# Both directions of a delta rule's block solution in one loop, its matmuls in 32x32 tiles by turns

## The chip, the cores and the metric

The kernel runs on one core of one Trainium2 chip. The metric is the device time of one execution in microseconds, from the first to the last instruction of the core, as the median of several runs.

## What is computed

Three blocks run one after the other on 256 tokens of 2048 channels. The first has a convolution, a chunked linear attention and an attention over a memory, the second a sparse attention, a gating unit and a wide layer, the third a latent attention and a delta rule in both directions of time. The change is in the third block's delta rule alone. Its core, per head of 64 channels, with 16 heads and 256 steps in each direction:

```python
def rwkv7_bidir_scan(r, w_f, w_b, k_f, k_b, v, kk, a_f, a_b):
    ...
    xs = (tm(r, r), tm(w_f, w_b), tm(k_f, k_b), tm(v, v), tm(-kk, -kk), tm(kk * a_f, kk * a_b))

    def step(st, inp):
        r_t, w_t, k_t, v_t, a_t, b_t = inp
        sa = jnp.einsum('dbhij,dbhj->dbhi', st, a_t)
        st = st * w_t[..., None, :] + sa[..., None] * b_t[..., None, :] + v_t[..., None] * k_t[..., None, :]
        y = jnp.einsum('dbhij,dbhj->dbhi', st, r_t)
        return st, y
    ...
    y = ys[:, 0] + ys[::-1, 1]
```

After it come a norm over each head, a bonus, a gate, and the layer `u_rwkv = (y_rwkv * silu(z_rwkv)) @ w_br_rwkv`.

## The kernel before, in words

**The main stream.** Nearly all of the work is linear layers. `run_stream` goes through their weights in a fixed order, in items of [128 rows, 512 columns]. ScalarE rounds an item to a high part `wh`, VectorE makes the remainder `wl`, and TensorE multiplies both with the high and low parts of the activations (`xh` and `xl`, of the rwkv results `yr0` and `yr1`) into the accumulators `acc`: three matmuls for each of the two blocks of 128 tokens, six an item. Six items' `wh` and `wl` exist at a time, and an item is split five items ahead of its matmuls (`LEAD`).

**Side work.** Everything else is written as generators ("sides") that give up control at each `yield`. Between the main products `pump` takes a step of each side whose last step should be through by then. What "should" means is set by the class `Issue`, a planner that runs at build time: it adds up, in microseconds of its own, what each engine has been given (a side matmul in 4-byte numbers costs `max(0.085, max(n, m) / 600 + 0.003)`). Before an item's matmuls `need` lets sides step on until the activations have been made by the planner's clock. So the order of every engine's instructions is fixed when the program is built; on the chip each engine takes its own in that order and waits where an operand is missing. A tile's results are evacuated (`finish`) before the next tile's `need`. Sides share four banks of PSUM (`bank`, `unbank`).

**The delta rule.** `job(g)` does 8 of the 16 heads, job 0 before job 1. Within blocks of 128 tokens the recurrence is a triangular system `u = w + (a b) u`, which is solved by four blocks of 32 tokens. `inverses` has made the inverses of the diagonal blocks (`J["tt"]`; the profile calls the tile `tl`), `scores` the products `ab`, and the state that enters the second block of 128 tokens is `zb`. `solve(J, d)` is one side for each direction `d`; both run at once and are interleaved by `pump`. For each of the direction's two blocks of 128 tokens (`n`), and each of the four blocks of 32 tokens in them (`e`, of quarter `q`):

- VectorE adds what earlier blocks gave (bank `pw`) to the rows `w` of `w0` (the profile calls it `w`);
- 8 matmuls, one a head, multiply `w` with the inverse into the quarter `q` of the bank `pu`, which both directions share under a lock per quarter; tile 32x32 at position (32 q, 32 q);
- ScalarE copies `pu` to `w`;
- `ab` products add the block's share to the quarters of `pw` still to come: in the first step (`e == 0`) two per head, one of 32 and one of 64 columns, in turn; in the second one of 64; in the third one of 32.

Between the two blocks of 128 tokens come 4 products with `bT` into another bank, which advance `zb`, and the flag `half`, for which `early` waits. `early` and `outputs` multiply the solution with `m` (tile `m0`), and `outputs` of job 1 norms, gates, transposes (`vy`) and splits the result into `yr1`. The main stream's layer `br1` (its first half, `br0`, takes job 0's `yr0`) is the first to read `yr1`.

Each engine instruction goes through one wrapper, so all have its line (283 before, 285 after).

Of the kernel before, what the change touches and what calls it, by code (L numbers as in the profile page):

```python
# [13 lines left out]
PSUM = bass.MemoryType.PSUM  # L14
AF = mybir.ActivationFunctionType
ALU = mybir.AluOpType
# [19 lines left out]
# tiles (the first so many of a layer) whose results come with the columns on the partitions:  # L36
# [128, 2, 256 tokens] in each of two banks
# [6 lines left out]
# ---------------------------------------------------------------- layout plan (shapes alone)  # L44
def stream_plan(blocks):
    """Tiles of the linear layers in the order in which they run:
    (key, j, source, first row, K chunks, first column, width)."""
# [63 lines left out]
class Narrow:  # L111
    """The result of a tile of a few columns, for which the weights are the stationary operand."""
# [5 lines left out]
def cut(plan):  # L118
    """Cuts the tiles into items of at most ITEM columns of SBUF, and these into DMA units."""
# [19 lines left out]
def col(v):  # L139
    """A vector over channels as [128, n / 128]."""  # L140
    return np.asarray(v).reshape(-1, 128).T


CVEC = {  # per-channel vectors, channel on the partition
# [33 lines left out]
ROWS = {  # vectors that are spread over the partitions  # L178
# [6 lines left out]
def shape_constants(block):  # L185
    """Constants of the shapes alone, [128, n] each."""
# [23 lines left out]
def bucket_onehot():  # L210
    """[32, 384]: the bucket of the distance 255 - c in column c; no bucket for negative distances."""
# [7 lines left out]
# ---------------------------------------------------------------- order of issue  # L219
class Issue:  # L220
    """Counts what each engine has been given (in microseconds, by the sizes of the operands), so that
    side work is issued between the main products about when its operands are there."""
# [16 lines left out]
    def take(self, eng, name, a, k):  # L239
# [3 lines left out]
        if eng == "PE":  # L243
# [3 lines left out]
            elif a[2].dtype == F32R:  # L247
                cost = max(n, 256) / 2400 + 0.003
            else:
                m = size(a[1])  # L250
                cost = max(0.085, max(n, m) / 600 + 0.003)
            self.t["PE"] += cost
# [42 lines left out]
# ---------------------------------------------------------------- the kernel  # L295
class Builder:
# [29 lines left out]
    # ---- memory  # L326
# [10 lines left out]
    def slotw(self, shape, name, keep=0, dtype=F32):  # L337
        """Side: a slot, once more than keep of them are free."""
# [14 lines left out]
    def keep(self, shape, name, dtype=F32):  # L353
        """A tile for as long as the block lasts."""
# [6 lines left out]
    def bank(self, n=1):  # L361
        """Waits for n banks of PSUM for side work, until they should have been read."""
# [2616 lines left out]
```

## Time and profile before

| | |
|---|---|
| median of 3 runs | 3649.19 us |
| lowest and highest | 3646.6 and 3651.16 us |
| span of the profiled execution | 3652.5 us |
| TensorE busy (matmul, weight load) | 3624.7 us (99%), 3110.4 us (85%) |
| VectorE, ScalarE, GpSimd busy | 67%, 52%, 4% |
| mean granted TensorE clock | 0.989 |

The profile is one execution of the program. Busy shares are means over the whole span, while the solution takes place in four stretches between 3072 and 3488 us: the first and the second block of 128 tokens of job 0 (3072 to 3114, 3125 to 3170), and those of job 1 (3388 to 3428, 3441 to 3488). What it costs there is read in the timeline.

### The profile page before, as it was taken

The page shows a single profiled execution, that of the slowest core. Times are in us where ns is not written, and L with a number is a line of the kernel's source. Part 1 is how long each engine was busy: PE and PEld are TensorE (multiplying, and loading weights), DVE is VectorE, ACT ScalarE, POOL GpSimd, SP SyncE. Part 2 cuts the span into 40 slices and gives each one's busy share as a digit, 9 for nine tenths or more (in the row PEclk, how much of TensorE's full clock was granted, in tenths as well). Part 3 has the DMA queues.
Part 4 walks back from the last instruction along what each step waited for, and adds up shares of the span by engine and source line. Part 5 has one row for each costly group of instructions (what it writes and reads, how often), then busy time and mean ns, then how long its engine had stood idle before and what let it go on. Part 6 is the DMA issues. An engine that isn't in the chain of part 4 may idle for free.

```text
span 3652.5 us, 56016 instructions
## 1 busy us (share of the span) xinstructions
PE 3624.7 (99%) x20498; PEld 3110.4 (85%) x20498; DVE 2453.4 (67%) x4453; ACT 1896.2 (52%) x3402; POOL 150.8 (4%) x141
## 2 busy tenths in 40 slices
PE   8999999999999999999999999999999999999998
PEld 7889988888988899888879898989888977877787
DVE  7598888886666665555855555555674786477485
ACT  6555556556544545655455454545555643353344
POOL 1000010010000001000200000000000000000010
PEclk9999999999999999999999999999999999999899
DMA  6555556676677665666755555555653555356365
GB/s 227 170 189 160 183 165 200 208 222 185 208 216 238 221 202 177 197 216 212 240 195 185 191 185 193 183 194 183 211 190 131 186 181 193 120 163 192 136 216 187
DMA packets 231772, 698.47 MB, mean 191 GB/s; under 512 B 40708, under 2 KB 51124, under 8 KB 229832
## 3 DMA queue, kind: packets, MB, share of 16 engines
q1 hardware_dynamic: 231496, 694.90, 58.9%
q8 instruction: 160, 2.62, 0.3%
q14 instruction: 116, 0.95, 0.1%
HBM read 661.22 MB, written 36.73 MB: 191 GB/s over the span
## 4 chain that ended last, share of the span: by engine, by line
PE 96%; DVE 2%; DMA 1%; ACT 1%; issue 0%; POOL 0%; SPq 0%; DVEq 0%; ACTq 0%
PE acc L283 85%; PE bank L283 11%; DVE wl L283 1%; DMA raw<-in_wstream_dram 1%; ACT wh L283 0%; DMA x<-f 0%; DMA sg<-z 0%; ACT junk L283 0%; DVE o L283 0%; DVE x L283 0%; DVE rsz L283 0%; DVE sg L283 0%; POOL mg L283 0%; SPq L283 0%; DVE mg L283 0%
## 5 line engine op out<-in xcount | busy, mean ns | idle before, releaser
L283 DVE TENSOR_TENSOR wl<-raw,wh 128x512 fp32r<-128x512 f32 x2290 | 1574.2, 703 | 1051.2 <-ACT wh L283 1037.9
L283 ACT ACTIVATE wh<-raw 128x512 fp32r<-128x512 f32 x2290 | 1424.0, 629 | 1553.5 <-PE acc L283 994.0
L283 PE MATMUL acc<-wh,xh 128*128 128x512 f32 x3328 | 1331.4, 400 | 8.5 <-ACT xh L283 5.0
L283 PE MATMUL acc<-wh,xl 128*128 128x512 f32 x3328 | 1302.2, 391 | 4.3 <-DVE xl L283 4.3
L283 PE MATMUL acc<-wl,xh 128*128 128x512 f32 x3328 | 1301.5, 391 | 0.9 <-DVE wl L283 0.9
L283 PEld LDWEIGHTS acc<-wh,xh 128*128 128x128 f32 x3328 | 629.1, 189 | 157.1 <-issue 21.0
L283 PEld LDWEIGHTS acc<-wh,xl 128*128 128x128 f32 x3328 | 628.7, 189 | 138.3 <-DVE xl L283 5.1
L283 PEld LDWEIGHTS acc<-wl,xh 128*128 128x128 f32 x3328 | 629.7, 189 | 124.6 <-DVE wl L283 2.5
L283 PE MATMUL acc<-xh,wh 128*128 128x256 f32 (+3 forms) x2224 | 637.3, 287 | 0.0
L283 PE MATMUL acc<-xh,wl 128*128 128x256 f32 (+3 forms) x2224 | 629.6, 283 | 0.0
L283 PE MATMUL acc<-xl,wh 128*128 128x256 f32 (+3 forms) x2224 | 629.5, 283 | 0.0
L283 PEld LDWEIGHTS acc<-xh,wh 128*128 128x128 f32 (+3 forms) x2224 | 423.9, 191 | 5.5 <-issue 4.0
L283 PEld LDWEIGHTS acc<-xl,wh 128*128 128x128 f32 (+3 forms) x2224 | 424.1, 191 | 1.1
L283 PEld LDWEIGHTS acc<-xh,wl 128*128 128x128 f32 (+3 forms) x2224 | 423.7, 191 | 0.4
L283 DVE SCALAR_TENSOR_TENSOR cacc<-u,cvec,cacc 128x226 f32<-128x226 f32 (+28 forms) x464 | 188.5, 468 | 0.0
L283 PE MATMUL bank<-ar,bk 64*128 64x128 f32 (+1 forms) x384 | 77.3, 328 | 0.0
L283 PEld LDWEIGHTS bank<-ar,bk 64*128 64x128 f32 x384 | 48.5, 186 | 19.3 <-issue 13.4
L283 ACT ACT_TABLE_LOAD x44 | 56.5, 1283 | 3.2 <-DVE mmx L283 1.6
L283 PE MATMUL bank<-w,ab 32*32 32x64 f32 (+1 forms) x512 | 54.5, 244 | 0.0
L283 PEld LDWEIGHTS bank<-w,ab 32*32 32x32 f32 (+1 forms) x512 | 38.6, 128 | 17.8 <-issue 6.2
L283 POOL TENSOR_TENSOR msh<-ev 128x508 f32<-128x508 f32 x8 | 10.1, 1261 | 1043.0 <-DVE ev L283 989.5
L283 ACT COPY w<-bank 32x512 f32<-32x512 f32 (+1 forms) x48 | 24.5, 511 | 50.7 <-PE bank L283 47.1
(420 smaller groups left out, 2292.0 us busy)
## 6 DMA issues: line engine op xcount, KB each, us to landing
raw<-in_wstream_dram SPq DMA_DIRECT2D x1133, 512.0 KB, 3.7
gate<-sg SPq DMA_DIRECT2D x40, 256.0 KB, 2.5
row<-in_rows_dram SPq DMA_DIRECT2D x38, 256.0 KB, 4.8
sg<-gate SPq DMA_DIRECT2D x24, 256.0 KB, 2.9
sg<-z SPq DMA_DIRECT2D x24, 256.0 KB, 3.0
z<-sg SPq DMA_DIRECT2D x20, 256.0 KB, 4.6
f<-x SPq DMA_DIRECT2D x16, 256.0 KB, 2.5
gt<-gate SPq DMA_DIRECT2D x16, 256.0 KB, 4.4
```

The source lines that it names most:

```text
L283: r = f(*a, **k)
```

## The change

`solve(J)` is one side for both directions. In each step the additions, products, copies and `ab` products of direction 0 and direction 1 are issued by turns; direction 0 works on quarter `e`, direction 1 on quarter `3 - e`. Each direction holds one bank `pw[d]` throughout: the products with the inverse go into the quarter of `pw[d]` that the addition has just read, and the state products into the same bank, so `pu`, its locks and `ps` go. Every `ab` product has a tile of 32x32, one per quarter still to come, and their group is cut in two in the first two steps. The flag `half` is set for both directions at once. The planner charges a matmul with a tile position half. Comments and docstrings were taken out too, which moves line numbers alone.

```diff
             else:
                 m = size(a[1])
                 cost = max(0.085, max(n, m) / 600 + 0.003)
+                if "tile_position" in k:
+                    cost /= 2
...
-            J["pu"], = yield from B.bank()
-            for d in range(2):
-                B.side(solve(J, d))
+            B.side(solve(J))
...
-            B.unbank(J["pu"])
...
-        def solve(J, d):
-            order = (0, 1) if d == 0 else (1, 0)
-            qs = (0, 1, 2, 3) if d == 0 else (3, 2, 1, 0)
-            ab, tt, w0 = J["ab"][d], J["tt"][d], J["w0"]
-            yield from B.wait(f"zb{d}{J['g']}")
-            zb, bT, pu = J["zb"][d], J["bT"][d], J["pu"]
-            for n, b in enumerate(order):
-                pw, = yield from B.bank()
...
-                for e, q in enumerate(qs):
-                    rows = slice(32 * q, 32 * q + 32)
-                    w = w0[rows, d, b]
+        def solve(J):
+            for d in range(2):
+                yield from B.wait(f"zb{d}{J['g']}")
+            ab, tt, w0, zb = J["ab"], J["tt"], J["w0"], J["zb"]
+            pw = yield from B.bank(2)
+            hs = [slice(h * 64, h * 64 + 64) for h in range(8)]
+            for n in range(2):
+                bs = (n, 1 - n)
...
+                for e in range(4):
+                    qs = (e, 3 - e)
+                    rows = [slice(32 * q, 32 * q + 32) for q in qs]
+                    ws = [w0[rows[d], d, bs[d]] for d in range(2)]
                     if n or e:
                         yield
-                        V.tensor_tensor(out=w, in0=pw[rows], in1=w, op=ALU.add)
+                        for d in range(2):
+                            V.tensor_tensor(out=ws[d], in0=pw[d][rows[d]], in1=ws[d], op=ALU.add)
                         yield
-                    yield from B.lock(f"pu{q}")
                     for h in range(8):
-                        T.matmul(pu[rows, h * 64:h * 64 + 64], tt[rows, 2 * h + b], w[:, h * 64:h * 64 + 64],
-                                 start=True, stop=True, tile_position=(32 * q, 32 * q))
-                    yield
-                    A.copy(out=w, in_=pu[rows])
-                    B.unlock(f"pu{q}")
-                    yield
-                    if e < 3:
-                        for h in range(8):
-                            for t0, m in ((32, 32), (64, 64)) if q == 0 else ((64, 32), (0, 64)) if q == 3 else (
-                                    ((64, 64),) if e == 1 and d == 0 else ((0, 64),) if e == 1 else
-                                    ((96, 32),) if d == 0 else ((0, 32),)):
-                                T.matmul(pw[t0:t0 + m, h * 64:h * 64 + 64], ab[rows, 2 * h + b, t0:t0 + m],
-                                         w[:, h * 64:h * 64 + 64], start=not n and e == 0 and h == 0, stop=e == 2,
-                                         tile_position=(32 * q, t0), skip_group_check=True)
-                B.unbank(pw)
+                        for d in range(2):
+                            T.matmul(pw[d][rows[d], hs[h]], tt[d][rows[d], 2 * h + bs[d]], ws[d][:, hs[h]], start=True,
+                                     stop=True, tile_position=(32 * qs[d], 32 * qs[d]), skip_group_check=True)
+                    yield
+                    for d in range(2):
+                        A.copy(out=ws[d], in_=pw[d][rows[d]])
+                    yield
+
+                    for h in range(8 if e < 3 else 0):
+                        if h == 4 and e < 2:
+                            yield
+                        for i in range(e + 1, 4):
+                            for d in range(2):
+                                t0 = 32 * (i, 3 - i)[d]
+                                T.matmul(pw[d][t0:t0 + 32, hs[h]], ab[d][rows[d], 2 * h + bs[d], t0:t0 + 32],
+                                         ws[d][:, hs[h]], start=not n and e == 0 and h == 0, stop=e == 2,
+                                         tile_position=(32 * qs[d], t0), skip_group_check=True)
                 if n == 0:
-                    ps, = yield from B.bank()
...
+                            T.matmul(pw[d][:, cs], J["bT"][d][:, cs], w0[:, d, d, cs], start=True, stop=True,
+                                     skip_group_check=True)
...
+            B.unbank(*pw)
+            J["done"] = [0, 1]
```

TensorE, first step of the solution's first block in job 0: the last main products ahead of the `ab` products (output, operands and output size; a name's number tells buffers apart). Before:

```order
L283 MATMUL acc_31066<-wh,xh 128x512
L283 MATMUL acc_31066<-wl,xh 128x512
L283 MATMUL acc_31066<-wh,xl 128x512
L283 MATMUL bank_31167<-w_29031,ab 32x64
L283 MATMUL bank_31167<-w_29031,ab 64x64
```
After:

```order
L285 MATMUL acc_31065<-wh,xh 128x512
L285 MATMUL acc_31065<-wl,xh 128x512
L285 MATMUL acc_31065<-wh,xl 128x512
L285 MATMUL bank_31166<-w_29031,ab 32x64
L285 MATMUL bank_31167<-w_29031,ab 32x64
```
Before, one direction's products of two sizes follow each other in one bank, eight pairs for each direction; now the two directions' banks take turns with products of one size, 24, three main products, and 24 more.

TensorE, end of job 1: the transposes of its normed results (`vy`) and the main products around them (`yr_33944` and `yr_33886` are job 0's half, `yr_35052` is job 1's). Before:

```order
L283 MATMUL acc_34828<-wl,yr_33944 128x512
L283 MATMUL acc_34828<-wh,yr_33944 128x512
L283 MATMUL bank_34862<-cst_80,vy 128x128 x4
L283 MATMUL acc_34827<-wh,yr_33944 128x512
L283 MATMUL acc_34827<-wl,yr_33944 128x512
L283 MATMUL acc_34827<-wh,yr_33944 128x512
```
After:

```order
L285 MATMUL acc_34962<-wh,yr_33886 128x512
L285 MATMUL acc_34962<-wl,yr_33886 128x512
L285 MATMUL acc_34962<-wh,yr_33886 128x512
L285 MATMUL bank_35054<-cst_80,vy 128x128 x4
L285 MATMUL bank_35061<-cst_80,vy 128x128 x4
L285 MATMUL acc_35068<-wh,yr_35052 128x512
```
The transposes of the two token blocks stood 9 main products apart, and 21 more products of job 0's half followed before the first of job 1's; now they stand together, straight ahead of the first product that reads `yr1`. From the last product with `m` to that one there were 147 main products, and there are 27.

VectorE at the same place: the first steps of the norm of job 1's results. Before:

```order
L283 TENSOR_TENSOR vy<-bank_34569,vy 128x512
L283 TENSOR_REDUCE yst<-vy 128x8
L283 TENSOR_SCALAR yst<-yst 128x8
L283 TENSOR_TENSOR wl<-raw,wh 128x512 x2
L283 TENSOR_TENSOR vy<-vy,yst 128x512
L283 TENSOR_TENSOR wl<-raw,wh 128x512
L283 TENSOR_TENSOR vy<-vy,yst 128x512
L283 TENSOR_TENSOR wl<-raw,wh 128x512 x2
L283 TENSOR_TENSOR mg<-acc_34508,sg 128x512
```
After:

```order
L285 TENSOR_TENSOR vy<-bank_34933,vy 128x512
L285 TENSOR_REDUCE yst<-vy 128x8
L285 TENSOR_SCALAR yst<-yst 128x8
L285 TENSOR_TENSOR wl<-raw,wh 128x512 x4
L285 TENSOR_TENSOR sg<-acc_34961,sg 128x512
L285 TENSOR_TENSOR sg<-acc_34962,sg 128x512
L285 TENSOR_TENSOR vy<-vy,yst 128x512 x2
L285 TENSOR_REDUCE yst<-tl 128x8
```
The mean's subtraction (`vy<-vy,yst`) stood between the splits of the main stream's weights; now it stands behind four of them and behind the evacuation of the tile (`acc_34961`, `acc_34962`) whose last main products are the last ahead of `yr1`, and the rest of the norm follows without a split in between.

## Rows read from the trace of the kernel before

**Rows 1.** The page: busy engines, the chain's shares, rounding of weights on ScalarE.
```profile
PE 3624.7 (99%) x20498; PEld 3110.4 (85%) x20498; DVE 2453.4 (67%) x4453; ACT 1896.2 (52%) x3402; POOL 150.8 (4%) x141
...
PE 96%; DVE 2%; DMA 1%; ACT 1%; issue 0%; POOL 0%; SPq 0%; DVEq 0%; ACTq 0%
...
L283 ACT ACTIVATE wh<-raw 128x512 fp32r<-128x512 f32 x2290 | 1424.0, 629 | 1553.5 <-PE acc L283 994.0
```

**Rows 2.** Matmuls by form: line, operands, tile, size, count, busy us, mean ns, idle.
```profile
L283 PE MATMUL bank<-w,tl 32*32 32x64 f32 x512 | 33.6, 223 | 0.0
L283 PE MATMUL bank<-w,ab 32*64 32x64 f32 x256 | 33.2, 251 | 0.0
```

**Rows 3.** Busy us over the solution's four stretches, of `tl` rows, then of `ab` rows.
```profile
sum 173.60, PE 33.60 PEld 29.49 DVE 0.00 ACT 0.00 POOL 0.00; mean PE 8.40 PEld 7.37 DVE 0.00 ACT 0.00 POOL 0.00
...
sum 173.60, PE 54.49 PEld 38.56 DVE 0.00 ACT 0.00; mean PE 13.62 PEld 9.64 DVE 0.00 ACT 0.00
```

**Rows 4.** Timeline of PE, job 0: start us, busy us, operands, tile, count of rows.
```profile
3072.24 1.78 PE L283 MATMUL bank<-w,tl 32*32 32x64 f32 x32
3073.95 0.50 PE L283 MATMUL acc<-wh,xh 128*128 128x512 f32 x1
3074.28 0.39 PE L283 MATMUL acc<-wl,xh 128*128 128x512 f32 x1
3074.51 0.40 PE L283 MATMUL acc<-wh,xl 128*128 128x512 f32 x1
...
3125.51 1.08 PE L283 MATMUL bank<-w,tl 32*32 32x64 f32 x16
3126.52 0.50 PE L283 MATMUL acc<-wh,xh 128*128 128x512 f32 x1
...
3130.78 3.89 PE L283 MATMUL bank<-w,ab 32*32 32x64 f32 x32
3134.60 1.59 PE L283 MATMUL bank<-w,tl 32*32 32x64 f32 x16
```

**Rows 5.** Timeline of PE where the two directions' products meet, job 0.
```profile
3165.36 0.21 PE L283 MATMUL bank<-w,tl 32*32 32x64 f32 x1
...
3165.41 0.21 PE L283 MATMUL bank<-w,tl 32*32 32x64 f32 x1
...
3165.50 0.27 PE L283 MATMUL bank<-w,ab 32*32 32x64 f32 x2
```

**Rows 6.** Half-clock windows, `acc` rows alone: us, PE busy (count), ..., PEclk; first, sum.
```profile
3080.38:3090.62 10.24, 4.78 (x11) 3.80 (x12) 0.00 (x0) 0.00 (x0) 0.50 0.37 154
...
sum 47.78, PE 23.11 PEld 16.50 DVE 0.00 ACT 0.00; mean PE 4.62 PEld 3.30 DVE 0.00 ACT 0.00
```

**Rows 7.** Timeline of PE at the end of job 1: after `m`, and first transposes.
```profile
3491.56 0.47 PE L283 MATMUL acc<-wh,xh 128*128 128x512 f32 x1
...
3519.66 0.60 PE L283 MATMUL bank<-cst,vy 128*128 128x128 f32 x4
```

**Rows 8.** Timeline of VectorE, then one row of ScalarE, in the norm of job 1.
```profile
3501.15 0.68 DVE L283 TENSOR_REDUCE yst<-tl 128x8 f32<-128x512 f32 x1
...
3503.97 0.68 DVE L283 TENSOR_REDUCE yst<-tl 128x8 f32<-128x512 f32 x1
...
3514.75 0.69 DVE L283 TENSOR_TENSOR vy<-vy,yst 128x512 f32<-128x512 f32 x1
3515.47 0.69 DVE L283 TENSOR_TENSOR vy<-vy,gh 128x512 f32<-128x512 f32 x1
3516.08 2.49 DVE L283 TENSOR_TENSOR wl<-raw,wh 128x512 fp32r<-128x512 f32 x4
...
3498.61 1.14 ACT L283 ACTIVATE tl<-vy 128x512 f32<-128x512 f32 x2
```

**Rows 9.** The first product after a wait of PE, and the half-clock window around it.
```profile
1862.73 0.79 PE L283 MATMUL acc<-wh,xh 128*128 128x512 f32 x1 [3.48 <-ACT wh L283]
...
1861.82:1868.65 6.83, 5.92 (x17) 4.59 (x18) 5.27 (x9) 4.92 (x11) 0.00 (x0) 0.50 0.47 148
```

More of the change, by code (lines that the diff above doesn't have):

```diff
@@ L2591, in solve @@
                 if n:
                     for c in range(4):
-                        T.matmul(pw[:, c * 128:c * 128 + 128], J["ar"][1][:, d, c, 0], zb[:, c], start=c == 0, stop=False,
-                                 skip_group_check=True)
-                for e, q in enumerate(qs):
-                    rows = slice(32 * q, 32 * q + 32)
-                    w = w0[rows, d, b]
+                        for d in range(2):
+                            T.matmul(pw[d][:, c * 128:c * 128 + 128], J["ar"][1][:, d, c, 0], zb[d][:, c], start=c == 0,
+                                     stop=False, skip_group_check=True)
@@ L2619, in solve @@
-                B.unbank(pw)
-                if n == 0:
-                    ps, = yield from B.bank()
-                    for c in range(4):
-                        cs = slice(c * 128, c * 128 + 128)
-                        T.matmul(ps[:, cs], bT[:, cs], w0[:, d, b, cs], start=True, stop=True)
-                    yield
-                    pv = ps.rearrange("p (c i) -> p c i", i=128)
-                    for i in range(2):
-                        rows = slice(64 * i, 64 * i + 64)
-                        z = zb[rows, :, rows]
-                        V.tensor_tensor(out=z, in0=pv[rows, :, rows], in1=z, op=ALU.add)
-                        V.tensor_tensor(out=z, in0=z, in1=J["sca"][rows, d].unsqueeze(2).to_broadcast([64, 4, 64]),
-                                        op=ALU.mult)
-                    B.unbank(ps)
+                    for h in range(8 if e < 3 else 0):
+                        if h == 4 and e < 2:
+                            yield
+                        for i in range(e + 1, 4):
+                            for d in range(2):
+                                t0 = 32 * (i, 3 - i)[d]
+                                T.matmul(pw[d][t0:t0 + 32, hs[h]], ab[d][rows[d], 2 * h + bs[d], t0:t0 + 32],
+                                         ws[d][:, hs[h]], start=not n and e == 0 and h == 0, stop=e == 2,
+                                         tile_position=(32 * qs[d], t0), skip_group_check=True)
@@ new lines, in solve @@
+                if n == 0:
+                    for d in range(2):
+                        for c in range(4):
+                            cs = slice(c * 128, c * 128 + 128)
+                            T.matmul(pw[d][:, cs], J["bT"][d][:, cs], w0[:, d, d, cs], start=True, stop=True,
+                                     skip_group_check=True)
+                    yield
+                    for d in range(2):
+                        pv = pw[d].rearrange("p (c i) -> p c i", i=128)
+                        for i in range(2):
+                            r = slice(64 * i, 64 * i + 64)
+                            z = zb[d][r, :, r]
+                            V.tensor_tensor(out=z, in0=pv[r, :, r], in1=z, op=ALU.add)
+                            V.tensor_tensor(out=z, in0=z, in1=J["sca"][r, d].unsqueeze(2).to_broadcast([64, 4, 64]),
+                                            op=ALU.mult)
@@ L2634, in solve @@
                     yield
-                    B.flag(f"half{d}{J['g']}")
-            J["done"].append(d)
+                    for d in range(2):
+                        B.flag(f"half{d}{J['g']}")
+            B.unbank(*pw)
+            J["done"] = [0, 1]
         def late_rows(J):
```

## The prediction

> **What bounds the kernel now.** I read the page from the top. TensorE (PE) is busy for 99% of the span, and 96% of the chain that ended last is its own matmuls [rows 1]; the reader is to see that nothing else comes near it. So the time is, to first order, the sum of PE's turns, and an edit pays by what it takes out of that sum, less the new waits it makes. The page hides what one turn costs, so I went on to the solution's matmuls by form: 512 rows on `tl` (the inverted diagonal blocks) and 512 on `ab` (what a solved block gives to later ones), 256 of these with 64 columns and as many with 32; a product of 4-byte numbers stands as two rows [rows 2]. By stretches they are busy for 33.6 + 54.5 = 88.1 us [rows 3].
>
> [...]
> One: 32 rows of one form take 1.71 us from their start to the next main product's and 16 take 1.01, some 0.056 us a row plus 0.11 for ending; but 32 rows in which 32- and 64-column tiles alternate take 3.82 [rows 4]. Each change of form costs about 0.13 us, at full clock. (Modelled ends reach past the next start: 1.78 against 1.71. So 88.1 busy us are 88.1 x 0.96 = 84 us of turns.)
> Two: where a product of one direction meets one of the other, in different quarters, five steps from start to start take 0.14 us, 28 ns each instead of 56 [rows 5]: two quarters run side by side.
> [...]
>
> **The change part by part.**
> *Products.* The `tl` products stay 256. The `ab` products go from 256 to 384, since what was one 64-column tile is now two of 32. That is 640 products, 1280 rows, against 1024. All have one form, and directions alternate, so that neighbours lie in different quarters of rows and of columns and write to different banks. By the order they stand in 28 groups of 32 rows and 8 of 48. I price each direction's half as a stream of its own with 56 ns a row: a group of 32 like 16 rows alone, 1.01, plus half a step, 1.04; a group of 48 is 8 x 0.056 more, 1.49. Sum: 28 x 1.04 + 8 x 1.49 = 41 us. Gain: 84 - 41 = 43 us, all on PE's path. The bounds: with nothing side by side, 1280 x 0.056 + 36 x 0.11 = 76, a gain of 8; a row at 27 ns, 40 us, is as low as any spacing in the trace lets me go. I take 41, because rows 5 show just this pairing, if only for a few starts in a row. What no row shows is a tile that moves by a column quarter inside its row quarter at every step, as `ab` now does. Its price lies between nothing and the form change's 0.13 us on 40 products per block (both directions at once), 4 x 40 x 0.13 = 21 us. I take nothing, as tile moves without a form change in rows 5 cost nothing, and keep 21 for the range.
> [...]
>
> *Groups.* Each group costs the main stream some 0.1 us at entry and 0.1 at exit (0.33 instead of 0.23 between the first two main products after one [rows 4]). I count 30 stretches in the order of before and 36 in that of after: +1.2 us.
>
> *Clock.* Without alternating forms I expect none of the five windows. Their share in the tiled rows is inside the 84; their share in main products is 51 x (0.453 - 0.23) = 11.4 us, a gain. Bound: all of them stay, 0.
>
> *Bank just read.* The `tl` product writes the quarter of the bank that VectorE has read to make the product's own operand, so it waits for nothing new; the state product writes a bank whose last reader made its operand too. Locks and `pu` go. Cost 0: the bank's reader is the operand's maker in each case. Two banks instead of up to four are held; PE is busy for 99% with them scarce [rows 1], so 0. The solution issues no DMA; stores of job 1's other steps shift among the weight loads on SP, which run four units of two items ahead, 8 x 6 x 0.23 = 11 us of products, and that hides them.
>
> *Waits inside the solution.* Both directions' copies on ScalarE now come before one group, and both additions on VectorE. The order puts 12 to 24 main products between, at least 12 x 0.23 = 2.8 us, against two operations of 0.6 to 0.7 us each, one unrelated split of 0.7 that may be running, and hand-overs of 0.1 to 0.2: 2.3 us. Cover suffices; if not, at most 0.7 us at 12 places, 8 us.
>
> *What is late next.* Since the planner now charges a tile half, and steps of both directions follow each other, the second job ends later in main products. Behind its last reads (`m`) stood 147 main products before the first that needs its results (`yr1`); now 27. By the order the PE then has only the transposes of `vy` left, and VectorE has, ahead of the norm, the split of the last weights and two evacuations (`sg<-acc`) that themselves wait for the last of the 27. So the chain starts when PE runs out. In before it was hidden: from 3491.56 (`m` done) to the transposes at 3519.66 PE ran main products [rows 7]. Priced from there: last split (ScalarE 0.63, VectorE 0.62 to 0.69, hand-overs) 1.5; two evacuations 1.2; mean subtracted 0.7; square on ScalarE, the pair 1.14, first one with hand-overs 0.9; two reductions with their roots, 2.82 each, 5.6; six products and sums, three dependent ones at 0.72 and three at 0.61, 4.0; transposes, copy, remainder 0.9 + 0.7 + 0.8 [rows 1, 8]. Sum 16.4, of which 0.4 is PE's own work: a wait of 16 us. Bounds 6 (only the six products and the transposes left) and 20 (VectorE behind). After a 3.5 us wait in before, the clock stood at 0.50 for 6.8 us, 5.9 of which had work [rows 9]: at half speed they lose 3 us. I add 3, bounds 0 and 6.
>
> **The sum.** The profiled execution spans 3652.5 us; the median of three runs is 3649.2, 3.3 lower, and I apply the difference to the median. -43 (products) - 11.4 (clock) + 1.2 (groups) + 16 + 3 (the wait) = -34: **3615 us**. Its own range: with a wait of 6, no clock loss and 40 us of products, 3601; with a wait of 20, a loss of 6 and 8 us of waits inside the solution, 3630.
>
> **The rivals.**
> *Turns without overlap* (slower). PE starts a product only when the one ahead in the other quarter is through, so spacing stays 56 ns, and groups of 48 rows then last as long as what pulled the clock down. Gain 8 only, clock unchanged, +1.2 + 19: 3649 - 8 + 20 = 3661. With the old clocks it decides from a spacing of (84 - 20 - 4) / 1280 = 47 ns on. For it: rows 5 are at most a handful of starts, perhaps fed from a queue. Against: they recur wherever the two directions meet.
> *Column moves drain PE*: +21, 3636. For it: the cost of form changes. Against: it is seen only with a change of form.
> *The clock still falls*: +11.4, 3626. Stretches stay small-tiled with three main products between the halves; but no stretch of one form lowered it before.
> *Partly side by side*, about 40 ns: 1280 x 0.040 + 4 = 55 us instead of 41: 3629; with the clock unchanged 3641.
>
> **How the numbers follow.** Forecast 0.62, clock still low 0.12, column drains 0.10, partly 0.08, no overlap 0.08. A measurement of this kernel tells about 0.2% from no change, 7 us, so faster means below 3642. All but the last and a little of the fourth lie there: faster 0.87, same 0.06, slower 0.07. The range leaves out the no-overlap case and the worst of the partial ones, whose ends are 3641 and 3661: 3601 to 3641.
>
> **What would show it.** Tiled rows by stretches busy for some 40 to 45 us in place of 88; starts 28 ns apart inside whole groups; no window at 0.50 between 3060 and 3480; and a new idle of about 16 us on PE ahead of the first `yr1` product, ended by VectorE, with a half-speed window right after. Busy time near 76 us would mean no overlap. If PE shows no idle at `yr1`, the chain ran earlier than the order suggests and the time is nearer 3596. What would make it wrong most: group spacing, since it carries 35 of the 54 us of gain.

## The result, and the profile after

The changed kernel takes 3603.07 us (3602.59 to 3603.35, four runs) where the kernel before takes 3650.18 (3646.6 to 3651.32): a ratio of 0.9872, 95% interval 0.986 to 0.9885, so 47 us or 1.3% faster. The forecast was 3615 with a range of 3601 to 3641. The profiled executions span 3601.6 us against 3652.5.

Of the page after, the line of busy engines and that of the chain, as in [rows 1]:

```profile
PE 3561.6 (99%) x20754; PEld 3063.9 (85%) x20754; DVE 2451.2 (68%) x4453; ACT 1896.3 (53%) x3402; POOL 149.0 (4%) x141
...
PE 97%; DVE 1%; DMA 1%; ACT 0%; issue 0%; SPq 0%; DVEq 0%; ACTq 0%
```

TensorE (PE) still bounds the kernel, and its busy time fell by 63 us, more than the span did. The solution's products by form, as in [rows 2] (busy us, mean ns):

```profile
L285 PE MATMUL bank<-w,tl 32*32 32x64 f32 x512 | 17.4, 216 | 0.0
L285 PE MATMUL bank<-w,ab 32*32 32x64 f32 x768 | 15.4, 218 | 0.0
```

They are busy for 32.8 us in 1280 rows, where 1024 rows were busy for 88.1 us [rows 3]. The timeline of PE in job 0 (start us, busy us, operands, tile, count of rows), as in [rows 4]:

```profile
3067.24 1.08 PE L285 MATMUL bank<-w,tl 32*32 32x64 f32 x32
3068.25 0.50 PE L285 MATMUL acc<-wh,xh 128*128 128x512 f32 x1
...
3071.21 0.73 PE L285 MATMUL bank<-w,ab 32*32 32x64 f32 x48
3071.88 0.50 PE L285 MATMUL acc<-wh,xh 128*128 128x512 f32 x1
...
3081.73 0.65 PE L285 MATMUL bank<-w,ab 32*32 32x64 f32 x32
3082.31 0.50 PE L285 MATMUL acc<-wh,xh 128*128 128x512 f32 x1
```

From the start of a group to the start of the next main product: 32 rows on `tl`, which lie on two tiles, take 1.01 us; 48 rows on `ab` on six tiles 0.66; 32 rows on four tiles 0.58. More rows in less time: what counts is how many rows fall to one tile, 16, 8 and 8. I call the sum of these steps over all tiled rows the tiled turns: 83.2 us in before, 30.3 in after. Inside a group the starts come in bunches: in a `tl` group two rows 6 to 7 ns apart, a pair mostly every 55 to 57 ns; in a group of 48 rows six within 33 ns, and the next six mostly 56 ns later. So each of the tiles in turn starts a row of its own about every 56 ns.

The clock and the end of job 1 (a stretch with PE's busy time and count, ..., granted clock, and then PE's rows):

```profile
3060.00:3455.00 395.00, 395.00 (x3058) 312.96 (x3057) 273.18 (x513) 180.45 (x316) 7.77 (x9) 1.00 0.57 187
3461.45:3478.52 17.07, 4.02 (x13) 3.34 (x14) 14.06 (x36) 2.46 (x4) 2.93 (x2) 0.50 0.25 90
```
```profile
3457.90 0.40 PE L285 MATMUL acc<-wh,yr 128*128 128x512 f32 x1
...
3474.50 1.94 PE L285 MATMUL bank<-cst,vy 128*128 128x128 f32 x8 [16.20 <-DVE vy L285]
3476.27 0.79 PE L285 MATMUL acc<-wh,yr 128*128 128x512 f32 x1
```

The solution's stretches run at 1.00 throughout, where five windows (stretches of a lower granted clock), 47.8 us in all, stood at 0.50 [rows 6]. Ahead of the transposes of `vy` PE waits 16.20 us for VectorE, and the clock is at 0.50 until 3478.5: eight transposes take 1.77 us to the next product instead of 0.7 (before's four take 0.35 at 1.00, from 3519.66 us on), and five main products 2.28 instead of 1.16 (five steps of 0.23 [rows 4]). VectorE during the wait (start us, busy us, operation, count):

```profile
3458.81 2.50 DVE L285 TENSOR_TENSOR wl<-raw,wh 128x512 fp32r<-128x512 f32 x4
3461.23 1.28 DVE L285 TENSOR_TENSOR sg<-acc,sg 128x512 f32<-128x512 f32 x2
3462.42 3.05 DVE L285 TENSOR_TENSOR vy<-vy,yst 128x512 f32<-128x512 f32 x2
3465.40 0.67 DVE L285 TENSOR_REDUCE yst<-tl 128x8 f32<-128x512 f32 x1
...
3468.20 0.68 DVE L285 TENSOR_REDUCE yst<-tl 128x8 f32<-128x512 f32 x1
...
3473.05 1.90 DVE L285 TENSOR_TENSOR vy<-vy,gh 128x512 f32<-128x512 f32 x3
```

It is the chain that the prediction had named: splits, two evacuations, the mean, two reductions 2.8 us apart, six products and sums. Not all of its parts have the forecast sizes (see below).

### The profile page after: what moved, and what is told of

Same layout as the page of the kernel before. It is cut to its first block, busy times and chain, and to the rows that moved or that the text cites. A ratio compares the mean times of both kernels' runs of the same rounds, so it can differ in the third digit from the quotient of the medians.

```text
span 3601.6 us, 56526 instructions
## 1 busy us (share of the span) xinstructions
PE 3561.6 (99%) x20754; PEld 3063.9 (85%) x20754; DVE 2451.2 (68%) x4453; ACT 1896.3 (53%) x3402; POOL 149.0 (4%) x141
## 4 chain that ended last, share of the span: by engine, by line
PE 97%; DVE 1%; DMA 1%; ACT 0%; issue 0%; SPq 0%; DVEq 0%; ACTq 0%
PE acc L285 87%; PE bank L285 10%; DVE wl L285 0%; DMA raw<-in_wstream_dram 0%; DMA x<-f 0%; ACT wh L285 0%; DVE vy L285 0%; DVE o L285 0%; DVE xl L285 0%; DVE rsz L285 0%; ACT junk L285 0%; DVE yst L285 0%; ACT xh L285 0%; DVE x L285 0%; SPq L285 0%
## 5 line engine op out<-in xcount | busy, mean ns | idle before, releaser
L285 ACT ACTIVATE junk<-x 128x512 bf16<-128x512 f32 x40 | 25.3, 631 | 36.7 <-DVE x L285 36.3
L285 PE MATMUL acc<-wh,yr 128*128 128x512 f32 x128 | 44.0, 408 | 0.0
L285 POOL TENSOR_TENSOR crstd<-crstd,u 128x256 f32<-128x256 f32 x14 | 21.8, 1560 | 358.6 <-DVE u L285 358.1
```

Of the source, the lines that this page charges most:

```text
L285: r = f(*a, **k)
```

## The experiments

Each ratio is to runs of the kernel before on the same chip, whose medians were 3649.6 us for e1 to e4, 3647.2 for e5 to e7, 3649.5 for e8 and e9, and 3654.0 for e10 and e11. "Wait" is PE's wait at the transposes of `vy`; "windows" are those at half clock that begin inside the solution's groups or within 1 us behind one (e5, e10 and e11 have one more of 3.4 us, some 40 us behind job 0's last group, which I leave out).

| kernel | us | ratio to before, 95% | tiled turns | wait | windows |
|---|---|---|---|---|---|
| before | 3649 | 1 | 83.2 | 0 | 5, 47.8 us |
| after | 3603.1 | 0.986 to 0.9885 | 30.3 | 16.2 | none |
| e1, no turns | 3620.1 | 0.9911 to 0.9936 | 47.4 | 16.2 | none |
| e2, two tiles in turn | 3610.4 | 0.9883 to 0.991 | 35.6 | 16.2 | none |
| e3, two widths | 3650.4 | 0.9991 to 1.0009 | 63.8 | 16.2 | 4, 44.4 us |
| e4, full charge | 3602.4 | 0.9861 to 0.9888 | 30.9 | 13.6 | none |
| e5, tiles alone | 3604.1 | 0.9863 to 0.9895 | 48.5 | 0 | none |
| e6, sooner | 3584.9 | 0.9814 to 0.9842 | 29.8 | 0.7 | none |
| e7, one apart | 3587.8 | 0.9822 to 0.9849 | 32.7 | 0 | none |
| e8, widths sorted | 3608.4 | 0.9875 to 0.9905 | 34.3 | 16.2 | none |
| e9, before sorted | 3626.0 | 0.9922 to 0.9947 | 63.1 | 0 | 4, 23.9 us |
| e10, thrice | 3684.0 | 1.0075 to 1.0112 | 91.8 | 16.2 | 9, 51.2 us |
| e11, thrice by turns | 3635.3 | 0.993 to 0.9963 | 58.8 | 16.2 | none |

**e1: the turns undone.** Inside a group, all of direction 0 and then all of direction 1 (`part` holds the four or eight heads of an `ab` group).

```diff
-                    for h in range(8):
-                        for d in range(2):
+                    for d in range(2):
+                        for h in range(8):
                             T.matmul(pw[d][rows[d], hs[h]], tt[d][rows[d], 2 * h + bs[d]], ws[d][:, hs[h]], ...
...
-                        for i in range(e + 1, 4):
-                            for d in range(2):
+                    for d in range(2):
+                        for h in part:
+                            for i in range(e + 1, 4):
```

> After's kernel, but inside each group of the solution's products all of direction 0 come first and then all of direction 1; the tiles stay 32x32, and nothing else moves. After's groups last 1.01 us (32 rows on `tl`), 0.66 (48 rows on `ab`), 0.58 (32) and 1.01 (32 of the third step). Theory (each tile is a stream of its own of 56 ns a row; what counts is how many different tiles stand among neighbours in the order): a `tl` group goes back to 1.71 us as before's 32 rows of one form, 16 x 0.70 = 11 us; the `ab` halves hold three, then two, tiles at a time instead of six and four, 8 x 0.45 + 8 x 0.45 = 7; the third step's group 4 x 0.7 = 3. In all +21 us over after, 3624 us, tiled turns 51 us instead of 30. Rival (the array takes products far out of order, so the order inside a group is of no account): no change, 3603. Second rival (only the turns of directions overlap, columns of one quarter do not): the `ab` halves go to 2.7 and 1.8 us, +40 us, 3643.

3620.1 us, 17.0 above after; tiled turns 47.4, 17.2 above. PE's timeline:

```profile
3066.51 1.78 PE L285 MATMUL bank<-w,tl 32*32 32x64 f32 x32
3068.21 0.50 PE L285 MATMUL acc<-wh,xh 128*128 128x512 f32 x1
...
3071.17 0.91 PE L285 MATMUL bank<-w,ab 32*32 32x64 f32 x48
3072.01 0.50 PE L285 MATMUL acc<-wh,xh 128*128 128x512 f32 x1
```

All sixteen `tl` groups are back at 1.71 us, before's price [rows 4]: +11.0. The `ab` halves of 48 rows take 0.84, not the 1.1 of the theory: I read this as PE beginning the second direction's tiles before the first direction's are through; single starts in before's trace show the like over four rows (last section). So the order counts, within a few rows. Both rivals are out.

**e2: two tiles in turn.** The column quarter moved to the outer loop, directions still by turns.

```diff
-                    for h in range(8 if e < 3 else 0):
-                        if h == 4 and e < 2:
-                            yield
-                        for i in range(e + 1, 4):
-                            for d in range(2):
+                    for part in ((range(4), range(4, 8)) if e < 2 else (range(8),) if e == 2 else ()):
+                        if part[0]:
+                            yield
+                        for i in range(e + 1, 4):
+                            for h in part:
+                                for d in range(2):
```

> After's kernel, but the `ab` products of a group run column quarter by column quarter: the two directions still take turns product by product, but only two tiles are in turn at a time instead of six or four. Theory (a tile is a stream of its own of 56 ns a row): a half group of 48 rows is three stretches of 8 rows a tile, 3 x 0.45 + 0.15 = 1.5 us, the price that the prediction gave it, instead of 0.66, and one of 32 rows 1.03 instead of 0.58: 8 x 0.84 + 8 x 0.45 = +10 us, 3613 us, and some less if PE takes a few rows ahead at each change of column. Rival (what shortened the groups is the small tile as such, not how many tiles take turns): no change, 3603.

3610.4 us, +7.3. A half group of 48 rows:

```profile
3074.46 1.16 PE L285 MATMUL bank<-w,ab 32*32 32x64 f32 x48
3075.54 0.50 PE L285 MATMUL acc<-wh,xh 128*128 128x512 f32 x1
```

1.09 us in place of 0.66, and 0.83 in place of 0.58 for 32 rows: 8 x 0.42 + 8 x 0.25 = 5.3 us of tiled turns; the other 2 us are within what executions differ by ahead of the solution: of the 9.0 us between the profiled executions 3.2 lie there. The solution starts at 3070.48 us in e2 and 3067.24 in after although PE's rows up to there stand in the same order. Among all the kernels here, which share that order, this start lies between 3065.4 (e5) and 3072.2 us (before). The same products on the same tiles are dearer when fewer tiles stand next to each other, and cheaper than pairs in a row would be (1.5), which I put down to one pair's end overlapping the next one's start.

**e3: two widths in after's loop.** In a block's first step the tiles of before, 32 and 64 columns, product by product.

```diff
+                        for h in part:
+                            for d in range(2):
+                                for t0, m in (((32, 32), (64, 64)), ((64, 32), (0, 64)))[d] if e == 0 else [...]:
+                                    T.matmul(pw[d][t0:t0 + m, hs[h]], ab[d][rows[d], 2 * h + bs[d], t0:t0 + m], ...
```

> After's loop, but in the first step of a block the `ab` products have before's tiles, one of 32 and one of 64 columns per head and direction, in turn (16 products in a half group instead of 24). Theory (a change of form empties the array, 0.13 us each at full clock, and stretches of such changes pull the clock down): the 8 half groups go from 0.66 to 3.8 us, +25 us, and half-clock windows come back between 3060 and 3480 us with some 11 us of loss in main products: 3603 + 25 to 36 = 3628 to 3639. Rival (the change costs only where neighbours lie in one quarter of the rows, so that turns of directions hide it): at most 2 us, 3605, no windows.

3650.4 us: this alone takes back the whole gain, and 11 us more than expected. Three of its half groups (the clock falls within the first and is low in the second), and a window:

```profile
3071.61 4.04 PE L285 MATMUL bank<-w,ab 32*32 32x64 f32 x32
3075.58 0.80 PE L285 MATMUL acc<-wh,xh 128*128 128x512 f32 x1
...
3077.16 6.04 PE L285 MATMUL bank<-w,ab 32*32 32x64 f32 x32
3083.14 0.80 PE L285 MATMUL acc<-wh,xh 128*128 128x512 f32 x1
...
3449.79 3.89 PE L285 MATMUL bank<-w,ab 32*32 32x64 f32 x32
3453.61 0.50 PE L285 MATMUL acc<-wh,xh 128*128 128x512 f32 x1
```
```profile
3075.20:3088.90 13.70, 13.70 (x52) 9.28 (x52) 5.03 (x6) 1.50 (x3) 0.00 (x0) 0.50 0.35 132
```

At full clock a half group of 16 products takes 3.82 us (the third), exactly before's price [rows 4], although directions take turns; at half clock 5.98. Tiled turns +33.6, main products +10. What was not expected is that half the groups would themselves run at half clock.

**e8: the same products, sorted by width.** One more loop outside, so that a half group has first all of 32 columns and then all of 64.

```diff
+                        for w in range(2 if e == 0 else 1):
+                            for h in part:
+                                for d in range(2):
+                                    for t0, m in [(((32, 32), (64, 64)), ((64, 32), (0, 64)))[d][w]] if e == 0 else [...]:
```

> The kernel of e3_two_widths (after's loop, tiles of 32 and of 64 columns in a block's first step), with the same products in another order: in each half group first all of 32 columns, then all of 64, so that the form changes once where it changed 16 times; directions still take turns. Theory (it is the change of form that costs, and what pulls the clock down): a half group lasts 16 rows on two tiles twice, 2 x 0.45, a change of 0.1 to 0.3 and 0.1 to 0.2 at its ends, 1.2 us instead of 3.8 to 6.0; no half-clock window between 3060 and 3455; 3603 + 8 x 0.55 = 3607 (3604 to 3611). Rival (a 64-column tile is slow as such, or small and mixed tiles within one stretch pull the clock down): the half groups stay above 2 us and windows come, 3620 to 3650.

3608.4 us, as the theory has it:

```profile
3069.80 1.25 PE L285 MATMUL bank<-w,ab 32*32 32x64 f32 x32
3070.97 0.50 PE L285 MATMUL acc<-wh,xh 128*128 128x512 f32 x1
```

1.17 us a half group, tiled turns 34.3, no window. A 64-column tile is not slow (1.17 us for the half group); changing the form at every product is (3.82 in e3). Nothing but the order of the 16 products in each half group lies between 3650 and 3608.

**e5: the tiles alone.** The kernel before with 32x32 tiles for all `ab` products; two sides, locks, banks, charges as before, no turns.

```diff
-                            for t0, m in ((32, 32), (64, 64)) if q == 0 else ((64, 32), (0, 64)) if q == 3 else (
-                                    ((64, 64),) if e == 1 and d == 0 else ((0, 64),) if e == 1 else
-                                    ((96, 32),) if d == 0 else ((0, 32),)):
+                            for t0 in ((32, 64, 96), (64, 96), (96,), ())[q] if d == 0 else ((), (0,), (0, 32), (0, 32, 64))[q]:
+                                m = 32
```

> The kernel before with one part of the change alone: every `ab` product has a 32x32 tile; two sides, locks, banks, planner and the order of everything else stay as before. Theory (a tile is a stream of its own; a change of form empties the array and brings the half-clock windows): the first steps' groups, 3.8 us at full clock and more at half, become some 1.0 us for 16 rows on each of three tiles, the others stay near 1.0; tiled turns go from 83 to some 53 us, main products gain the 10 us that they lost at half clock, and nothing waits ahead of `yr1`: 3650 - 30 - 10 = 3610, though the directions take no turns. Rival (the turns of directions carry the gain): the `ab` groups of one direction run row by row at 56 ns, 2.7 us for 48 rows and 1.9 for 32; -8 and +7 against before, the clock -10: 3639.

3604.1 us, the time of the whole change within the error (the intervals of the two ratios overlap). Both directions' products of a first step, which stand back to back:

```profile
3069.38 1.80 PE L283 MATMUL bank<-w,ab 32*32 32x64 f32 x96
3071.11 0.50 PE L283 MATMUL acc<-wh,xh 128*128 128x512 f32 x1
```

96 rows in 1.73 us, the time of 32 rows on two tiles without turns (1.71): 16 rows on the fullest tile, twice. Tiled turns 48.5, 35 below before and 18 above after; main products from the solution's start on 8 us below before; no wait at `vy`. So the small tiles alone give 43 us (3647.2 to 3604.1 on this chip), which is 35 and 8. The turns give another 18, and the one loop takes them back at the end of job 1.

**e9: before with two loops exchanged.** The cheapest repair that the theory of e3 suggests: eight products of one width, then eight of the other.

```diff
-                        for h in range(8):
-                            for t0, m in ((32, 32), (64, 64)) if q == 0 else ...
+                        for t0, m in ((32, 32), (64, 64)) if q == 0 else ...
+                            for h in range(8):
```

> The kernel before with two loops exchanged and nothing else: in a direction's first step all eight products of one tile width come first, then all eight of the other; the tiles, the sides, the banks and the planner's times stay. Theory (change of form): of 15 changes in a first step's group one is left; 32 rows on two tiles one after the other, 1.71 as before's rows of one form, and 0.1 to 0.3 for the change, some 1.9 us where e5_tiles_alone has 0.86; 8 x 1.0 = 8 us more than e5, no half-clock windows between 3060 and 3480: 3612 (3608 to 3618), so about four fifths of what the whole change gave. Rival (the 64-column tiles themselves cost, or the clock falls whatever the order): 3630 to 3650.

3626.0 us: half of the gain, and 14 us worse than expected. Both directions' first step, and the clock behind it:

```profile
3073.91 4.22 PE L283 MATMUL bank<-w,ab 32*32 32x64 f32 x64
3078.06 0.67 PE L283 MATMUL acc<-wh,xh 128*128 128x512 f32 x1
```
```profile
3078.25:3081.60 3.35, 3.35 (x9) 2.61 (x9) 0.65 (x2) 0.63 (x1) 0.00 (x0) 0.50 0.96 396
3426.40:3440.00 13.60, 13.60 (x78) 11.14 (x76) 2.50 (x4) 2.64 (x5) 0.00 (x0) 0.50 0.13 40
```

64 rows in 4.15 us, 2.08 a direction where I had reckoned 1.9; tiled turns 63.1 in place of 57. And four half-clock windows are back, 24 us, with only one to three changes of form in the group ahead of each; the same group of 4.15 us in job 1 has none. My cause of the windows, alternating forms, was in doubt.

**e10 and e11: the clock by itself.** After's groups on `tl` are issued three times over; nothing is left out, and each writes the same again. In e10 direction by direction, in e11 by turns.

```diff
+                    for _ in range(3):
                         for d in range(2):
                             for h in range(8):
```

> A measurement of the clock, not of a part of the change: after's kernel, in which each group of products with the inverse is issued three times over (each writes the same result again), direction by direction: 96 rows of one form with never more than one tile in turn. A group lasts 1.71 us for each 32 rows, some 5.0 us, 16 x 4.0 = 64 us more than in after. Theory F (changes of form pull the clock down, as the prediction had it): no half-clock window between 3060 us and the end of the solution, 3603 + 64 = 3667 (3660 to 3672). Theory L (a stretch of several us in which small tiles run one at a time pulls it down, of whatever form; e9 had windows with one change per group behind stretches of 4.15 us): windows at most of the groups, each making the rest of a stretch and the main products behind it half as fast, 3690 to 3730.

> The same threefold groups, but by turns of the directions as in after: 96 rows on two tiles, 48 on each, 48 x 0.056 + 0.11 = 2.8 us, 16 x 1.8 = 29 us more than in after: 3632 without half-clock windows (theory F). Theory L: the same 96 rows in little more than half the time may stay above what pulls the clock down, 3632 too; windows here and none in e10 would speak against both.

e10 takes 3684.0 us, slower than before, and e11 3635.3. A group of e10 and the stretch right behind it, then a group of e11:

```profile
3066.87 4.58 PE L285 MATMUL bank<-w,tl 32*32 32x64 f32 x96
3071.37 0.50 PE L285 MATMUL acc<-wh,xh 128*128 128x512 f32 x1
```
```profile
3071.75:3075.14 3.39, 3.39 (x10) 2.62 (x9) 1.71 (x2) 0.99 (x2) 0.00 (x0) 0.50 1.02 430
```
```profile
3070.68 2.87 PE L285 MATMUL bank<-w,tl 32*32 32x64 f32 x96
3073.48 0.50 PE L285 MATMUL acc<-wh,xh 128*128 128x512 f32 x1
```

In e10 nine of the sixteen groups, stretches of at least 4.5 us of a single form, have a window at 0.50 that begins inside them or within 0.6 us behind. Theory F is out: no change of form is needed. Theory L is right in kind, but its time was too high, as the clock did not fall at every group: at seven of the eight in job 0, and at two of the eight in job 1. In e11 the same 96 rows take 2.80 us, and no window follows. What else the stretches of e3, e9 and e10 have in common, beyond small tiles one after the other for some microseconds, these runs don't tell, and it stays open.

**e4: the planner's charge.** Before's charge put back.

```diff
-                if "tile_position" in k:
-                    cost /= 2
```

> After's kernel with before's planner charge: a tiled product is charged in full, not half. The prediction put job 1's late end down to the half charge and to the directions' steps that follow each other. Theory A (the half charge has a part in it): with the full charge job 1 ends earlier in main products, and the 16 us wait ahead of `yr1` shrinks to some 5: 3592. Theory B (it is the loop alone: two additions and two copies behind each other in each step, and one wait more per group): the wait stays 14 to 17 us, the time 3601 to 3605.

```profile
3475.19 1.94 PE L283 MATMUL bank<-cst,vy 128*128 128x128 f32 x8 [13.61 <-DVE vy L283]
```

3602.4 us, the same as after within the error; the wait is 13.6 instead of 16.2. The half charge is at most a small part of why job 1 ends late: 27 main products stand between the last product with `m` and the transposes in after, 30 here.

**e6: the steps sooner.** Each of the loop's steps is due 0.9 us sooner by the planner's clock, and the `ab` groups are not cut in two.

```diff
+                        B.clock.done -= 0.9
                         yield
...
-                        if h == 4 and e < 2:
-                            yield
```

> After's kernel with the solution's steps due 0.9 us sooner by the planner's count, and the `ab` groups not cut in two, so that 6 to 9 main products stand between a step's parts where 12 to 15 stood (in after's trace an operand is there 0.9 to 1.7 us ahead of the group that reads it). Job 1 then ends some 210 main products earlier, 117 of them behind its last products with `m`. Theory (the wait ahead of `yr1` is the price of the longer loop alone, and with it goes the half clock behind it): no wait at the transposes of `vy`; 16.2 us of wait and 2 to 4 of half clock go, some 3 us of short waits inside the solution come: 3603 - 16 = 3587 (3583 to 3592). Rival (the steps need the products between them: PE then waits inside the solution what it saves at its end): 3600 to 3610.

```profile
3072.29 1.19 PE L285 MATMUL bank<-w,ab 32*32 32x64 f32 x96
3073.41 0.50 PE L285 MATMUL acc<-wh,xh 128*128 128x512 f32 x1
```
```profile
3430.47 0.63 PE L285 MATMUL bank<-cst,vy 128*128 128x128 f32 x4 [0.74 <-DVE vy L285]
```
```profile
3060.00:3570.00 510.00, 508.78 (x3590) 409.11 (x3590) 362.73 (x667) 244.79 (x427) 14.06 (x12) 1.00 0.59 194
```

3584.9 us, 18 below after and 62 below before on its chip. The wait and the half clock behind it are gone; inside the solution PE waits 0.4 us in all. The loop had been given more time than it needs: in after, operands lay ready 0.9 to 1.7 us ahead of most groups. The run changes two things at once, the due times and the cut, and does not tell their shares. This is the best version of the study.

**e7: one group apart.** Direction 1 runs one group behind, so that `tl` products of one direction take turns with `ab` products of the other, and the two directions' copy and addition lie on different engines. Its core:

```diff
+                for p in range(8):
+                    now = [(d, p - d) for d in range(2) if 0 <= p - d < 7]
+                    for h in range(8):
+                        for d, k in now:
+                            (rest if k % 2 else own)(d, n, k // 2, h)
```

> Another loop: direction 1 runs one group of products behind direction 0, so that the `tl` products of one take turns with the `ab` products of the other, and ScalarE's copy for one lies beside VectorE's addition for the other; steps due 0.9 us sooner as in e6. Theory (a group lasts as long as its fullest tile): 16 rows on the fullest tile in each of 8 groups a block, 8 x 1.01 = 8.1 us a block against 7.55 in after, tiled turns 32.5 us; no wait ahead of `yr1`: 3588 (3583 to 3594), the same as e6 within its error or 2 us above it. Rival (`tl` and `ab` products of one row quarter, which meet in two groups a block, do not run side by side): 0.9 us more in 8 groups, 3595.

```profile
3069.36 0.23 PE L285 MATMUL bank<-w,ab 32*32 32x64 f32 x3
3069.38 0.21 PE L285 MATMUL bank<-w,tl 32*32 32x64 f32 x1
3069.41 0.23 PE L285 MATMUL bank<-w,ab 32*32 32x64 f32 x3
3069.43 0.21 PE L285 MATMUL bank<-w,tl 32*32 32x64 f32 x1
```

3587.8 us, tiled turns 32.7, where 3588 and 32.5 were expected. Four tiles start one row each, three of them `ab` and one `tl`, and each its next some 0.05 us later. The rule of the fullest tile predicts a loop that had not been run; that copy and addition lie side by side gains nothing, as PE waits for neither: its waits on a bank in e7 are 1.6 and 0.6 us, both for other tiles.

## Why the prediction was right, and where it was off

The sign came from the right place: PE's turns, less a new wait. That the time lies within the range is in part luck: its lower end, 3601, stood for a wait of 6 us with products no cheaper than 40, and what came was a wait of 16.2 with products of 30.3.

In the profiled executions the span falls by 50.8 us. Tiled turns -53.0, half-clock main products -11.5, wait +16.2, clock behind it +2.2, two waits of 0.9 and 0.6 us behind before's job 1 that went with the order -1.5, the groups' ends +1.6: -46.0. From the start of the solution on the two executions differ by 45.8. The other 5.0 us are not of the change: the rows of PE, VectorE and ScalarE ahead of the solution stand in the same order in both, and its first group starts at 3072.24 us in before and 3067.24 in after (PE's waits up to there sum to 13.3 and 10.9 us, the windows at 0.50 to 23.9 and 13.7). The medians differ by 47.

- *Products, 84 to 41: the step that failed.* Measured 83.2 to 30.3. "I price each direction's half as a stream of its own with 56 ns a row" holds for `tl` groups (1.04 forecast, 1.01 measured), but the stream belongs to a tile, not to a direction; and starts are not 28 ns apart, but in bunches, one row for each tile. Six tiles in turn take 0.66 us for 48 rows, not 1.49, and four 0.58 for 32, not 1.04: 8 x 0.83 + 8 x 0.46 = 10.3 of the 11 us missed. What e2 gives when only two tiles are in turn, 1.09, is nearer to my price. The lower bound fell too: "as low as any spacing in the trace lets me go" was a bound on what the trace had happened to contain; 0.66 us for 48 rows is 14 ns a row. (Its 40 us go with 28 ns a row; 27 would give 38.6.)
- *Column moves, 0 of 21:* nothing, confirmed by the same rows. The rivals "without overlap", "partly" and "column moves drain PE" are out, and so is "the clock still falls": 1.00 throughout the solution.
- *Where the gain lies.* I wrote that group spacing by turns "carries 35 of the 54 us". It doesn't: e5 has no turns and gives 43 us. In e5 35 us come off the tiled turns (the changes of form, the half clock that some of them ran under, and three tiles of one direction side by side) and 8 off the main products. I had seen the first two in [rows 4, 6], and then credited the gain to the wrong edit. The turns are worth 17 (e1) to 18 us (e5 against after).
- *Clock, -11.4:* size right (-11.5), cause too narrow. Of before's five windows four begin while alternating forms run, 2.6 to 5.4 us behind the start of their group, and one (3134.99 us) 0.4 us behind such forms; the 51 main products in them took 23.1 us, 0.453 each, where the step at 1.00 is 0.23 [rows 4, 6]. Forms that alternate at every product do bring windows (four of 44.4 us in e3, and none in e8), but they are not needed: one form for 4.5 us brings windows too (nine in e10), and sorting the widths in before does not remove them all (four in e9). My evidence for the forms, that "no stretch of one form lowered it before", held no such stretch longer than 1.82 us.
- *Groups +1.2, bank just read 0, waits inside the solution 0:* from the solution's start on a main product at full clock takes 239.3 ns on the mean where it took 238.3, 1.6 us over the 1587 of them, near the +1.2. Nothing in after's trace speaks against the other two; PE is busy for all of the 395 us. The hand-overs of 0.1 to 0.2 us that I set against the cover were an estimate; in before VectorE starts a split 0.03 us after ScalarE's end (3498.74 and 3498.71 us).
- *Wait 16, clock 3:* 16.2 and 2.2 measured, on the chain that was named, but that 16 met 16.2 is luck. Up to the transposes I had summed 13.9 us (1.5 + 1.2 + 0.7 + 0.9 + 5.6 + 4.0), and the whole 16.2 lie there. From the end of PE's last product ahead of the wait, at 3458.30, it is 2.9 us to the evacuations and not 1.5, since four splits stand ahead of them, and the mean with the square takes 3.0 and not 1.6. The 2 us put down to the transposes, copy and remainder brought no wait. Of the two reasons given for the late end the half charge has at most a small part (e4: 2.6 us of wait, the same time). The other is the loop: e5 keeps the two sides and has no wait, and with the loop's steps due sooner and its groups uncut the wait goes (e6). How much of it comes from the two additions and two copies in a row and how much from the cut is not shown.

## What to carry to other kernels

Price small matmuls by the fullest tile, as long as all tiles take turns: rows on it times its own pace, plus the ends of the group (here some 56 ns a row: 16 rows 1.01 us, 8 rows 0.58 to 0.66). Order products so that neighbours lie on different tiles (e1 without turns took 17 us more) and the form never changes from one to the next; if forms must mix, sort them (a half group took 3.82 us in e3 and 1.17 in e8). When a loop joins two independent chains, count what its steps now stand behind, all the way to the last reader: here 18 us of turns were won in the loop and 18 lost at its end, and due times moved by 0.9 us, with groups left whole, kept the gain without the loss. A lower bound taken from the smallest spacing in a trace only bounds what that trace contained.

## What the runs showed of the hardware that was not expected

- Products of 32x32 tiles run side by side also within one quarter of the rows: with three tiles a direction, 48 rows of one direction last as long as 16 rows on one tile (e5: 96 rows in 1.73 us, 32 rows in 1.71).
- PE starts a few rows of the next tile before the last one's are through: in before's group at 3072.24 us, 16 rows on one tile and then 16 on another, starts are mostly 56 ns apart up to the thirteenth row, then 5, 50, 30, 26, 30, 26 and 30, and then 56 again. Each further stretch of 8 rows on other tiles costs 0.25 us (1.09 and 0.83 in e2, 0.58 in after), not the 0.45 of 8 rows at 56 ns.
- The granted clock fell to 0.50 while PE was busy without a gap: in e10 inside or right behind nine of sixteen groups of 96 rows on one tile at a time, 4.5 us long or more, never behind the 1.71 us groups of e1 nor behind the same 96 rows by turns of two tiles in 2.80 us (e11).
